# Modulation sums moved ahead of the mixers, and x normalised a tile every seven units

## The chip, the cores and the metric

The kernel runs on one core of one Trainium2 chip. The metric is device time in microseconds (us) of one execution; lower is better. The engines are named as the profile names them: PE (TensorE matmuls) with its weight loads PEld, DVE (VectorE), ACT (ScalarE), POOL (GpSimd), SP (SyncE, which issues DMAs).

## The reference

A decoder trunk of two layers on 256 positions of width 1024, all in float32. Each layer has three sub-layers: a SwiGLU feed-forward, a mixer (even layer: pooling beside differential attention; odd layer: a chunkwise mLSTM), and a second SwiGLU. Each sub-layer has an RMS norm whose shift and scale, and a residual gate, come from a conditioning vector c:

```python
def modnorm(x, g, shift, scale):
    return rmsnorm(x, g) * (1 + scale[:, None, :]) + shift[:, None, :]
...
for l in range(DEPTH):
    mod = (c_act @ w_mod[l] + b_mod[l]).reshape(B, N_SUB, 3, D_MODEL)
    shift, scale, gate = mod[:, :, 0], mod[:, :, 1], mod[:, :, 2]
    h = modnorm(x, norm_g[l, 0], shift[:, 0], scale[:, 0])
    x = x + 0.5 * gate[:, 0, None, :] * swiglu(h, w_ffn_gate[l, 0], w_ffn_up[l, 0], w_ffn_down[l, 0])
    h = modnorm(x, norm_g[l, 1], shift[:, 1], scale[:, 1])
    ...                                       # y = even_mixer(h, ...) or odd_mixer(h, ...)
    x = x + gate[:, 1, None, :] * y
    h = modnorm(x, norm_g[l, 2], shift[:, 2], scale[:, 2])
    x = x + 0.5 * gate[:, 2, None, :] * swiglu(h, w_ffn_gate[l, 1], w_ffn_up[l, 1], w_ffn_down[l, 1])
return rmsnorm(x, final_g)
```

So beside the layers' own matrices there is a modulation: 2 x 9 x 1024 dot products of length 1024 with silu(c).

## The kernel before

x lies transposed: eight tiles of 128 channels by 256 positions. All weights are cut into blocks of 128 by 128 and stand in memory in the order of use. One block is a **unit**; 16 units are a **chunk** of 1 MB, 8 units a **half**. A unit is three matmuls (mm3, lines 341 to 343): the weight's high part by x's high part, low by high, high by low, because both are split into a rounded high part and a remainder to keep float32 accuracy. The 160 chunks run in this order: feed-forward 1 (chunks 0 to 32, of which 0 to 21 are gate and up, 22 to 32 down), even mixer (33 to 40 input blocks, 41 to 44 output), feed-forward 2 (45 to 77, down from 67), feed-forward 3 (78 to 110, down from 100), odd mixer (111 to 122, 123 to 126), feed-forward 4 (127 to 159). In the profiled execution they begin at 17.7, 212.5, 301.7, 491.1, 679.3 and 795.3 us.

`split_to` (line 286) is called from each unit and stays two halves ahead (`look`): it asks SP for the next chunk (line 294), has ACT round a half into wh (line 299) and DVE subtract it into wl (line 300). wh and wl have four buffers each, the raw chunks five.

The **modulation** is summed on DVE: `mod_chunk` (line 242) loads two rows of w_mod blocks (1 MB, tile rawm, line 249) into the same five raw buffers, and `mod_sums` (line 260) makes two sums of 128 x 1024 products (line 267), always directly behind the second half of the chunk in front of which the load was asked for. How many of the 72 loads have been asked for by which chunk is told by the table `MOD_POINTS`, between whose points `mod_schedule` draws straight lines; 8 are made by hand at the start. So chunks 22 to 32, for instance, come with 8 loads.

A new stage begins before x's statistics are known. The last residual of the old stage (`residual`, line 460) at once writes xh and xl, x times the scale column, and the first blocks (`early`: 2 x `NEARLY` of them, so 10) are multiplied by these raw tiles. Two extra columns carry the shift, so their matmuls are 258 columns wide, and the result must be multiplied by the positions' factor `rext` when it leaves PSUM: DVE does so (tile t, line 512, in a feed-forward; tile ti, line 618, in a mixer). `stats_lane` (line 421) runs beside the units: 15 units into the stage the sum of squares is turned into the factor, 7 units later it is spread over the partitions, and from then on a tile of x is normalised every 4 units (`norm_x`, line 442: a product on DVE into xn, a rounding on ACT and a remainder on DVE into xs). Blocks that are not early read xs and are 256 columns wide. The blocks are swept with the last tile of x late for the first two (`sweep`, line 62): these two go over seven tiles each before they need the eighth.

Within a stage small generators (heads, gates, pooling) are stepped at given unit counts. In the odd mixer lf, col and dg are small columns of the gates' chain, each made on DVE (lines 798, 804, 822) and read by PE (lines 801, 808, 827); `head_qk` (line 853) multiplies a head's scores by their decay on DVE (line 866) before PE goes on in the same bank (line 868).

## Time and profile before

| | us |
|---|---|
| three runs | 993.95, 998.08, 998.33 |
| their median | 998.08 |
| the profiled execution | 998.09 |
| its span in the profile | 996.4 |

In a window's row each engine has its busy time and the number of instructions. Matmuls are pipelined, so that of PE not the busy time but the number of matmuls in a window tells the pace. A row of the waits tells which engine's instruction was late for which other one, summed over a window. Of one instruction the profile gives a duration; where instructions follow each other closely, the next one may start a little before the end of the one before, so start to start is the better measure of a queue.

### The profile page before, as it was taken

The page shows a single profiled execution, that of the slowest core. Times are in us where ns is not written, and L with a number is a line of the kernel's source. Part 1 is how long each engine was busy: PE and PEld are TensorE (multiplying, and loading weights), DVE is VectorE, ACT ScalarE, POOL GpSimd, SP SyncE. Part 2 cuts the span into 40 slices and gives each one's busy share as a digit, 9 for nine tenths or more (in the row PEclk, how much of TensorE's full clock was granted, in tenths as well). Part 3 has the DMA queues.
Part 4 walks back from the last instruction along what each step waited for, and adds up shares of the span by engine and source line. Part 5 has one row for each costly group of instructions (what it writes and reads, how often), then busy time and mean ns, then how long its engine had stood idle before and what let it go on. Part 6 is the DMA issues. An engine that isn't in the chain of part 4 may idle for free.

```text
span 996.4 us, 19641 instructions
## 1 busy us (share of the span) xinstructions
PE 973.5 (98%) x8032; PEld 958.8 (96%) x8032; DVE 758.1 (76%) x1201; ACT 528.0 (53%) x872; POOL 217.9 (22%) x223
## 2 busy tenths in 40 slices
PE   7999999999999999999999999999999999999996
PEld 6899999999999999999999999999899999999996
DVE  5979998989879876777798676788867988555452
ACT  3475544448766544444465444445767655444441
POOL 4953220110112322211122222001010113222011
PEclk9999999999999999999999999999999999999998
DMA  9978888875846766766758766676565746565521
GB/s 341 317 295 318 328 329 319 341 284 206 298 155 246 271 245 254 277 252 235 290 182 291 288 245 248 269 293 258 200 223 185 280 171 244 205 229 175 187 105 43
DMA packets 36093, 247.18 MB, mean 248 GB/s; under 512 B 4001, under 2 KB 4385, under 8 KB 7458
## 3 DMA queue, kind: packets, MB, share of 16 engines
q1 hardware_dynamic: 35856, 245.81, 66.7%
q8 instruction: 63, 1.03, 0.4%
q14 instruction: 28, 0.23, 0.1%
q10 hardware_dynamic: 146, 0.11, 0.0%
HBM read 244.86 MB, written 1.05 MB: 247 GB/s over the span
## 4 chain that ended last, share of the span: by engine, by line
PE 82%; DVE 9%; ACT 3%; issue 3%; POOL 1%; DVEq 0%; ACTq 0%; POOLq 0%
PE one L343 26%; PE one L341 26%; PE one L342 26%; DVE wl L300 3%; DVE rawm L267 3%; ACT wh L299 1%; DVE xs L447 1%; POOL hr L401 1%; DVE xn L445 1%; PE one L418 0%; DVE xl L587 0%; DVE t L512 0%; DVE h L490 0%; ACT L488 0%; PE one L842 0%
## 5 line engine op out<-in xcount | busy, mean ns | idle before, releaser
L300 DVE TENSOR_TENSOR wl<-raww,wh 128x1024 fp32r<-128x1024 f32 x320 | 395.5, 1239 | 162.4 <-ACT wh L299 161.1
L299 ACT ACTIVATE wh<-raww 128x1024 fp32r<-128x1024 f32 x320 | 337.2, 1056 | 226.7 <-PE one L343 197.3
L341 PE MATMUL one<-xs,wh 128*128 128x256 f32 x976 | 275.3, 282 | 0.0
L342 PE MATMUL one<-xs,wl 128*128 128x256 f32 x976 | 272.9, 280 | 1.0 <-DVE wl L300 1.0
L343 PE MATMUL one<-xs,wh 128*128 128x256 f32 x976 | 273.1, 280 | 0.0
L341 PE MATMUL one<-hid,wh 128*128 128x256 f32 x832 | 233.7, 281 | 0.2 <-ACT hid L601 0.2
L343 PE MATMUL one<-hid,wh 128*128 128x256 f32 x832 | 233.7, 281 | 0.0
L342 PE MATMUL one<-hid,wl 128*128 128x256 f32 x832 | 233.3, 280 | 0.0
L342 PE MATMUL one<-xh,wl 128*128 128x258 f32 (+1 forms) x752 | 207.5, 285 | 3.2 <-DVE wl L300 2.9
L341 PE MATMUL one<-xh,wh 128*128 128x258 f32 (+1 forms) x752 | 208.1, 287 | 1.8 <-ACT xh L585 1.8
L343 PE MATMUL one<-xl,wh 128*128 128x258 f32 (+1 forms) x752 | 204.6, 283 | 0.0
L493 POOL TENSOR_TENSOR hid<-h,hid 128x256 fp32r<-128x256 f32 x88 | 123.3, 1402 | 340.1 <-ACT hid L492 340.1
L342 PEld LDWEIGHTS one<-xs,wl 128*128 128x128 f32 x976 | 183.6, 188 | 1.4 <-DVE wl L300 1.2
L341 PEld LDWEIGHTS one<-xs,wh 128*128 128x128 f32 x976 | 183.0, 187 | 1.2 <-issue 1.0
L343 PEld LDWEIGHTS one<-xs,wh 128*128 128x128 f32 x976 | 183.1, 188 | 0.0
L341 PEld LDWEIGHTS one<-hid,wh 128*128 128x128 f32 x832 | 156.8, 188 | 0.4 <-ACT hid L601 0.4
L343 PEld LDWEIGHTS one<-hid,wh 128*128 128x128 f32 x832 | 156.6, 188 | 0.2 <-DVE hid L602 0.2
L342 PEld LDWEIGHTS one<-hid,wl 128*128 128x128 f32 x832 | 156.7, 188 | 0.0
L267 DVE CUSTOM_DVE_ANT_0 rawm<-rawm,cact,pk 128x1024 f32<-128x1024 f32 x112 | 150.5, 1371 | 0.0
L342 PEld LDWEIGHTS one<-xh,wl 128*128 128x128 f32 x752 | 140.6, 191 | 5.4 <-DVE wl L300 5.2
L341 PEld LDWEIGHTS one<-xh,wh 128*128 128x128 f32 x752 | 140.3, 191 | 4.1 <-ACT xh L585 2.3
L343 PEld LDWEIGHTS one<-xl,wh 128*128 128x128 f32 x752 | 138.8, 189 | 0.2 <-DVE xl L587 0.2
(222 smaller groups left out, 727.0 us busy)
## 6 DMA issues: line engine op xcount, KB each, us to landing
raww<-wst SPq DMA_DIRECT2D x152, 1024.0 KB, 4.8
rawm<-mst SPq DMA_DIRECT2D x71, 1024.0 KB, 4.9
raww<-wst SPq DMA_DIRECT2D x16, 512.0 KB, 6.4
xa<-xT SPq DMA_DIRECT2D x2, 512.0 KB, 4.7
rawm<-mst SPq DMA_DIRECT2D x2, 512.0 KB, 7.4
outT<-fin SPq DMA_DIRECT2D x3, 256.0 KB, 2.8
pk<-pack SPq DMA_DIRECT2D x1, 416.0 KB, 6.9
outT<-fin SPq DMA_DIRECT2D x2, 128.0 KB, 2.3
```

The source lines that it names most:

```text
L267: nc.vector.tensor_tensor_reduce(out=ri, in0=ri, in1=cact, scale=factor, scalar=first, op0=ALU.mult, op1=ALU.add, accum_out=modc[n // KT][ ...
L299: nc.scalar.activation(whs[i], src, AF.Copy)
L300: ins = nc.vector.tensor_tensor(out=wls[i], in0=src, in1=whs[i].bitcast(F32), op=ALU.subtract)
L341: nc.tensor.matmul(out, lhsT=wh, rhs=rh, start=start, stop=False, skip_group_check=skip)
L342: nc.tensor.matmul(out, lhsT=wl, rhs=rh, start=False, stop=False, skip_group_check=skip)
L343: nc.tensor.matmul(out, lhsT=wh, rhs=rl, start=False, stop=stop, skip_group_check=skip)
L401: nc.gpsimd.tensor_tensor(out=r, in0=v, in1=mhalf[:, 0:width], op=ALU.pow)
L445: nc.vector.scalar_tensor_tensor(out=xn, in0=x[k], scalar=a, in1=r, op0=ALU.mult, op1=ALU.mult)
L447: nc.vector.scalar_tensor_tensor(out=to[1], in0=xn, scalar=b, in1=to[0].bitcast(F32), op0=ALU.add, op1=ALU.subtract)
L493: nc.gpsimd.tensor_tensor(out=hl[:, 0:T], in0=h, in1=hh[:, 0:T].bitcast(F32), op=ALU.subtract)
```

## The change

Three constants change:

```diff
-NEARLY = 5
+NEARLY = 6
...
-MOD_POINTS = ((8, 8), (41, 32), (72, 44), (104, 56), (124, 68), (145, 72))
+MOD_POINTS = ((8, 8), (20, 18), (33, 31), (45, 32), (78, 47), (111, 68), (145, 72))
...
         for k in range(KT):
-            yield 4
+            yield 7
             norm_x(k, rext[:, 0:T], A_cols[key][:, k:k + 1], shift[:, k:k + 1], xs[k])
```

By the tables, the loads that are asked for in front of the chunks of each stage are:

| chunks | stage | before | now |
|---|---|---|---|
| 0 to 7 | feed-forward 1, start | 8 | 8 |
| 8 to 21 | feed-forward 1, gate and up | 9 | 11 |
| 22 to 32 | feed-forward 1, down | 8 | 11 |
| 33 to 44 | even mixer | 8 | 1 |
| 45 to 66 | feed-forward 2, gate and up | 8 | 10 |
| 67 to 77 | feed-forward 2, down | 4 | 5 |
| 78 to 99 | feed-forward 3, gate and up | 9 | 14 |
| 100 to 110 | feed-forward 3, down | 5 | 7 |
| 111 to 126 | odd mixer | 9 | 2 |
| 127 to 148 | feed-forward 4, gate and up | 4 | 3 |

Twelve blocks of a stage instead of ten are multiplied raw, and the eight tiles of x are normalised over 56 units instead of 32.

Three places show what moves. In the fences, wl is the low part of a half chunk, rawm<-...cact the two sums of a load (the row `mod_... 128x1` behind each only stores it), xa the residual sum into x.

The first is DVE's queue in the first down part. Before, from the first half of chunk 27 to the second of chunk 28:

```order
L300 TENSOR_TENSOR wl_2160<-raww_2157,wh_2159 128x1024
L461 SCALAR_TENSOR_TENSOR xa<-one_2082,mod_122,xa 128x256
L300 TENSOR_TENSOR wl_2198<-raww_2157,wh_2197 128x1024
L392 SCALAR_TENSOR_TENSOR xl_93<-xa,acol_2062,xh_85 128x256
L395 TENSOR_TENSOR xl_98<-mod_123,xh_90 128x2
L300 TENSOR_TENSOR wl_2230<-raww_2227,wh_2229 128x1024
L300 TENSOR_TENSOR wl_2268<-raww_2227,wh_2267 128x1024
L267 ISA rawm_2225,mod_125<-rawm_2225,cact,pk 128x1024
L267 ISA mod_125 128x1
```

Now, from the first half of chunk 27 to the first of chunk 28:

```order
L300 TENSOR_TENSOR wl_2174<-raww_2171,wh_2173 128x1024
L300 TENSOR_TENSOR wl_2212<-raww_2171,wh_2211 128x1024
L267 ISA rawm_2169,mod_126<-rawm_2169,cact,pk 128x1024
L267 ISA mod_126 128x1
L267 ISA rawm_2169,mod_127<-rawm_2169,cact,pk 128x1024
L267 ISA mod_127 128x1
L461 SCALAR_TENSOR_TENSOR xa<-one_2192,mod_122,xa 128x256
L368 SCALAR_TENSOR_TENSOR acol_3631<-mod_127,pk 128x1
L300 TENSOR_TENSOR wl_2246<-raww_2243,wh_2245 128x1024
```

Chunk 27 had no load in front of it, and the splits of chunks 27 and 28 followed each other with only a residual and its remainders between; now a load's two sums stand behind each chunk's splits, as for all chunks from 16 to 33.

The second is DVE's queue at the start of feed-forward 2, ahead of the split for the first half of chunk 50 (the last row in both; t is a raw block's evacuation, xs and xn are halves of a tile's normalisation). Before:

```order
L300 TENSOR_TENSOR wl_4156<-raww_4116,wh_4155 128x1024
L447 SCALAR_TENSOR_TENSOR xs_112<-xn_4128,mod_126,xs_111 128x256
L447 SCALAR_TENSOR_TENSOR xs_114<-xn_4144,mod_126,xs_113 128x256
L267 ISA rawm_4114,mod_128<-rawm_4114,cact,ghalf 128x1024
L267 ISA mod_128 128x1
L267 ISA rawm_4114,mod_128<-rawm_4114,cact,ghalf 128x1024
L267 ISA mod_128 128x1
L512 TENSOR_TENSOR t_4185<-one_4113,rext 128x258
L512 TENSOR_TENSOR t_4185<-one_4154,rext 128x258
L300 TENSOR_TENSOR wl_4200<-raww_4197,wh_4199 128x1024
```

Now:

```order
L490 SCALAR_TENSOR_TENSOR h_4095<-t_4090,sg_4093 128x256
L447 SCALAR_TENSOR_TENSOR xs_106<-xn_4114,mod_126,xs_105 128x256
L300 TENSOR_TENSOR wl_4138<-raww_4102,wh_4137 128x1024
L445 SCALAR_TENSOR_TENSOR xn_4144<-xa,acol_3631,rext 128x256
L512 TENSOR_TENSOR t_4169<-one_4101,rext 128x258
L300 TENSOR_TENSOR wl_4186<-raww_4183,wh_4185 128x1024
```

The two sums and the two remainders that stood between the second half of chunk 49 and that split now come behind it; a product and one evacuation are left.

The third is DVE's queue in the odd mixer, around the scores of head 3 (line 866). Before:

```order
L300 TENSOR_TENSOR wl_9368<-raww_9365,wh_9367 128x1024
L399 TENSOR_SCALAR hv_9319<-dss_9310 128x2
L908 TENSOR_TENSOR hr_9321<-hr_9321,dr_9309 128x2
L300 TENSOR_TENSOR wl_9433<-raww_9365,wh_9432 128x1024
L866 SCALAR_TENSOR_TENSOR hid_9410<-one_9407,hid_9082 128x256
L871 TENSOR_TENSOR hid_9414<-hid_9250,hid_9083 128x128
```

Now:

```order
L399 TENSOR_SCALAR hv_9347<-dss_9338 128x2
L908 TENSOR_TENSOR hr_9349<-hr_9349,dr_9337 128x2
L300 TENSOR_TENSOR wl_9461<-raww_9393,wh_9460 128x1024
L267 ISA rawm_9391,mod_137<-rawm_9391,cact,ghalf 128x1024
L267 ISA mod_137 128x1
L866 SCALAR_TENSOR_TENSOR hid_9438<-one_9435,hid_9114 128x256
L267 ISA rawm_9391,mod_137<-rawm_9391,cact,ghalf 128x1024
L267 ISA mod_137 128x1
L871 TENSOR_TENSOR hid_9442<-hid_9280,hid_9115 128x128
```

The scores' product stood directly behind a split; now one of a load's two sums stands between them.

## Rows read from the trace of the kernel before

**Rows 1.** The profile's page: busy time of two engines (us, share of the span, instructions), and the chain that ended last by engine, as shares of the span.

```profile
PE 973.5 (98%) x8032; PEld 958.8 (96%) x8032; DVE 758.1 (76%) x1201; ACT 528.0 (53%) x872; POOL 217.9 (22%) x223
...
PE 82%; DVE 9%; ACT 3%; issue 3%; POOL 1%; DVEq 0%; ACTq 0%; POOLq 0%
```

**Rows 2.** Busy time of the engines in windows of the span (from:to in us, length, then busy us and instructions of PE, PE's weight loads, DVE, ACT and POOL, the granted clock, the DMA engines' share, GB/s). They are, in this order, feed-forward 1's gate and up blocks from chunk 8 on; its down part; the even mixer's input blocks; feed-forward 2's gate and up; its down part; feed-forward 3's gate and up; the odd mixer's input blocks.

```profile
74.00:150.34 76.34, 76.34 (x647) 76.34 (x646) 70.77 (x98) 39.91 (x60) 22.13 (x18) 1.00 0.85 324
150.34:212.54 62.20, 62.20 (x531) 62.20 (x529) 54.63 (x82) 29.22 (x38) 6.17 (x7) 1.00 0.84 320
212.54:273.63 61.09, 60.52 (x487) 57.06 (x485) 55.33 (x119) 44.63 (x114) 6.48 (x5) 1.00 0.71 257
...
301.73:428.80 127.07, 126.07 (x1066) 125.86 (x1065) 100.16 (x147) 67.03 (x101) 33.37 (x24) 1.00 0.69 254
428.80:491.14 62.34, 62.34 (x531) 62.34 (x529) 45.45 (x63) 28.80 (x37) 6.61 (x7) 1.00 0.67 254
491.14:616.96 125.82, 125.82 (x1066) 125.82 (x1065) 97.70 (x146) 65.33 (x98) 31.90 (x23) 1.00 0.71 259
...
679.31:772.57 93.26, 90.63 (x715) 85.93 (x714) 70.37 (x165) 63.11 (x137) 5.44 (x6) 1.00 0.59 214
```

**Rows 3.** Waits of PE (engine and line, who ended the wait: us in total, times, longest us) in four windows, in this order: 212.54 to 301.73 us (even mixer), 300 to 335 (start of feed-forward 2), 679 to 773 (odd mixer), 795 to 825 (start of feed-forward 4).

```profile
PE one L710 <- ACT hid L705: 0.6, 1, 0.6
PE one L341 <- ACT hid L601: 0.2, 1, 0.2
...
PE one L342 <- DVE wl L300: 1.0, 1, 1.0
...
PE one L868 <- DVE hid L866: 1.7, 1, 1.7
PE one L827 <- DVE dg L822: 0.4, 1, 0.4
PE one L808 <- DVE col L804: 0.3, 1, 0.3
PE one L801 <- DVE lf L798: 0.2, 1, 0.2
...
PE one L342 <- DVE wl L300: 1.3, 1, 1.3
```

**Rows 4.** DVE in order of time, 327 to 333 us, around the wait at the start of feed-forward 2 (start us, duration us, engine, line, operation, out<-in, how many).

```profile
327.08 1.36 DVE L447 SCALAR_TENSOR_TENSOR xs<-xn,mod,xs 128x256 fp32r<-128x256 f32 x2
328.36 1.27 DVE L267 CUSTOM_DVE_ANT_0 rawm<-rawm,cact,ghalf 128x1024 f32<-128x1024 f32 x1
...
329.57 1.27 DVE L267 CUSTOM_DVE_ANT_0 rawm<-rawm,cact,ghalf 128x1024 f32<-128x1024 f32 x1
...
330.78 0.74 DVE L512 TENSOR_TENSOR t<-one,rext 128x258 f32<-128x258 f32 x2
331.45 1.21 DVE L300 TENSOR_TENSOR wl<-raww,wh 128x1024 fp32r<-128x1024 f32 x1
332.58 0.47 DVE L490 SCALAR_TENSOR_TENSOR h<-t,sg 128x256 f32<-128x256 f32 x1
```

**Rows 5.** Groups of equal instructions over the whole span (line, engine, operation, tiles and shapes, count | busy us, mean ns of one | idle time ahead of them and what ended it).

```profile
L299 ACT ACTIVATE wh<-raww 128x1024 fp32r<-128x1024 f32 x320 | 337.2, 1056 | 226.7 <-PE one L343 197.3 <-issue 17.3 <-DMA raww<-wst 6.5
...
L392 DVE SCALAR_TENSOR_TENSOR xl<-xa,acol,xh 128x256 fp32r<-128x256 f32 x40 | 31.6, 796 | 3.1 <-ACT xh L391 2.9
...
L445 DVE SCALAR_TENSOR_TENSOR xn<-xa,acol,rext 128x256 f32<-128x256 f32 x40 | 17.9, 478 | 0.0
...
L512 DVE TENSOR_TENSOR t<-one,rext 128x258 f32<-128x258 f32 x30 | 11.7, 416 | 0.7 <-ACT rext L429 0.7
```

**Rows 6.** DVE in order of time in the odd mixer, at two places: 701 to 703 us and 747 to 749 us (in brackets the idle time ahead of the instruction and what ended it).

```profile
701.19 1.28 DVE L267 CUSTOM_DVE_ANT_0 rawm<-rawm,cact,pk 128x1024 f32<-128x1024 f32 x1
...
702.87 0.16 DVE L798 SCALAR_TENSOR_TENSOR lf<-gt,ln 128x8 f32<-128x8 f32 x1
...
747.82 1.23 DVE L300 TENSOR_TENSOR wl<-raww,wh 128x1024 fp32r<-128x1024 f32 x1 [1.91 <-ACT wh L299]
748.97 0.42 DVE L866 SCALAR_TENSOR_TENSOR hid<-one,hid 128x256 f32<-128x256 f32 x1
```

**Rows 7.** Two windows of three chunks each in the gate and up part of feed-forward 3: its third to fifth chunk, read raw and 258 columns wide, and three later chunks of 256 columns (columns as in rows 2).

```profile
503.64:520.89 17.25, 17.25 (x147) 17.25 (x146) 17.25 (x32) 12.24 (x21) 5.18 (x4) 1.00 0.54 196
526.54:543.49 16.95, 16.95 (x147) 16.95 (x146) 13.51 (x19) 8.32 (x12) 5.20 (x4) 1.00 0.86 309
```

**Rows 8.** The DMA queue: the queue's own waits for the sums over the whole span (us in total, times, longest us); from issue to landing of the weight chunks that line 294 asks for between 140 and 215 us; and GB/s in 40 equal slices of the first down part (150.34 to 212.54 us, so 1.55 us a slice).

```profile
SPq L294 <- DVE mod L267: 100.2, 41, 4.4
...
DMA to landing us min/median/max: 4.7/5.1/6.4
...
GB/s 395 316 369 379 253 21 248 432 411 332 353 395 421 126 221 421 416 406 416 126 63 385 348 427 232 432 400 411 306 390 285 427 432 200 0 227 437 427 300 211
```

**Rows 9.** DVE in order of time: the residual of the first down part's last tile, whose last matmul ends at 212.54 us (columns as in rows 4).

```profile
213.33 0.47 DVE L461 SCALAR_TENSOR_TENSOR xa<-one,mod,xa 128x256 f32<-128x256 f32 x1
```

**Rows 10.** The sums of line 267 in two windows, 74 to 150.34 us (gate and up of feed-forward 1) and 679.31 to 772.57 us (odd mixer): count, then ns of one as least/median/most, first and last start, shape.

```profile
L267 DVE CUSTOM_DVE_ANT_0 rawm<-rawm,cact,pk x12: 1274/1516/1768, 107.7 to 149.2; 128x1024 f32<-128x1024 f32 x12
...
L267 DVE CUSTOM_DVE_ANT_0 rawm<-rawm,cact,pk x14: 1276/1278/1284, 688.0 to 771.5; 128x1024 f32<-128x1024 f32 x14
```

## The prediction

> **What bounds the kernel now.** The page first: TensorE (PE) is busy for 98% of the span, and the chain of waits that ended last goes through PE for 82% and through VectorE (DVE) for 9% [rows 1]. PE's busy share alone proves little, since matmuls overlap, so the second view is the stages: in the down projections (150 to 213 us and 429 to 491 us, 11 weight chunks each) PE issues 531 matmuls in 62.2 to 62.3 us, which is 5.65 us a chunk whatever DVE does beside it, and the granted clock is 1.00 throughout [rows 2]. The kernel is therefore an even stream of 160 chunks that only loses time where PE waits for another engine. The third view lists those waits [rows 3]. At the start of feed-forward 2 (300 to 335) PE waits 1.0 us for the low half of a weight split, at the start of feed-forward 4 (795 to 825) 1.3 us, in the odd mixer 1.7 + 0.4 + 0.3 + 0.2 = 2.6 us, in the even mixer 0.6 + 0.2 = 0.8 us. Together that is **5.7 us**, and it is all that an edit to DVE's order can win after the start-up, which the change leaves alone (both tables begin with 8 loads by chunk 8).
>
> DVE is the engine that can lose time. It holds its busy share at 70.8 of 76.3 us (93%) in the gate and up part of feed-forward 1 and at 54.6 of 62.2 us (88%) in its down part; in the odd mixer it is at 70.4 of 93.3 us [rows 2]. The change moves work from the latter to the former.
>
> **The price of a modulation load.** One load is 1 MB on the DMA queue and two sums on DVE. A sum takes 1.27 us by its row, but the next instruction starts 1.21 us after it (328.36, 329.57, 330.78) [rows 4], so I use 2.4 us for the pair. A split costs 1.13 us from start to start (331.45 to 332.58) [rows 4], one product or addition of normalising a tile of x 0.48 us by its row [rows 5], about 0.40 us back to back.
>
> **Part 1, fewer sums in the mixers.** By the tables the mixers' 28 chunks carry 3 loads in place of 17. In the odd mixer 14 sums become 4, so DVE loses 10 x 1.21 = 12.1 us of its 70.4. The wait of 0.2 us for lf goes with that, since a sum of 1.2 us stands directly ahead of the end of its chain (701.19) [rows 6]. The waits for col and dg (0.3 and 0.4 us) stay: what stands ahead of them are splits and normalised tiles, and the slower pace puts more of these beside that chain. The longest, 1.7 us for the scores of head 3 (L866), stays too: DVE idles 1.91 us for the high half of a weight split, takes the low half in 1.23 us (747.82) and only then turns to L866 [rows 6], and no sum is in that queue. In the changed order one sum stands between them. I price that at +0.3 us, bounds 0 and the whole sum of 1.2 us. In the even mixer 14 of 16 sums leave (8 loads become 1); what waits there is a power on POOL and a scaling on ScalarE behind DVE's statistics, of which I take half: 0.4 us. Gain of this part: 0.2 + 0.4 - 0.3 = 0.3 us.
>
> **Part 2, x normalised every 7 units.** Around 330 us a pair of sums, the last normalised tiles and two evacuations stand directly ahead of the split that PE waits for [rows 4]. In the changed order only one product and one evacuation are between that split and the one before, and the two sums of the next load come after it. That is 2.4 us of DVE less ahead of a wait of 1.0 us, so the wait goes. In feed-forward 4 the load falls ahead of the stage's own rush, and its 1.3 us go as well. Gain 2.3 us; bounds 0 (the delayed work makes the next split late in its place) and 2.3. The last tile of x is due at 15 + 7 + 8 x 7 = 78 units and is first read at unit 96 (before: 54 and 80), so PE has 18 units of 0.353 us, 6.4 us, of cover: no wait.
>
> **Part 3, twelve raw blocks instead of ten.** A raw block's matmuls are 258 columns wide. Three chunks of them take 17.25 us, three chunks of 256 columns 16.95 us, with 147 matmul records in both windows [rows 7]: 0.1 us a chunk. Two more blocks are one more chunk in each of five stages: **+0.5 us on PE**, bare. DVE gets ten more evacuations of 0.42 us by their rows [rows 5], hidden by its idle time (27 of 127 us in feed-forward 2's gate and up part, [rows 2]); without cover 4.2 us.
>
> **Part 4, more sums in the stages in front.** Chunks 8 to 21 get 11 loads instead of 9: DVE 70.8 + 2 x 2.4 = 75.6 of 76.3 us. Chunks 22 to 32 get 11 instead of 8: 54.6 + 7.2 = 61.8 of 62.2 us. DVE is full, not over. Chunks 78 to 99 get 14 instead of 9: 97.7 + 12.0 = 109.7 of 125.8; covered by the same slices' idle time, price 0, bounds 0 and 1.0 (the wait at 330 us, [rows 3]).
> What no row shows is one load for every chunk, 18 times running (chunks 16 to 33). Five buffers of 1 MB hold both kinds, so weight chunk c can only be asked for when the sums of the load two chunks earlier are done. The queue's own waits show this already: 100.2 us for sums, 41 times [rows 8]. Then it must land, 4.7, 5.1 or 6.4 us (least, median, most) in this stretch [rows 8], and be rounded by ScalarE in 1.06 us [rows 5]. So from one pair of sums to the split two chunks on: 0.1 + 5.1 + 1.06 = 6.3 us. From there DVE needs two splits, a pair of sums and one product, 5.1 us, in chunks 16 to 21, and 5.65 with the residuals in 22 to 33 (the 61.8 us above). Two chunks per 11.4 and 11.95 us are 5.70 and 5.98 us a chunk, 0.05 and 0.33 over PE's pace: 6 x 0.05 + 12 x 0.33 = 4.3 us behind at the end. Cover: a high half may start when PE leaves the half four earlier, 3 x 2.83 = 8.5 us before it is due, less 1.06 + 1.13, so 6.3 us. At the median PE does not starve. But the residual of the last tile comes late by the same amount: before, it ran 0.8 us after the stage's end (213.33 against 212.54) [rows 9]; PE reads that tile 14 units or 4.9 us into the mixer, and the residual (0.4 us), its rounding (some 0.5, as a product) and the remainder (0.8) [rows 5] with their hand-overs need about 2 us, so 2.9 us are free. 4.3 less the 1 us by which DVE was ahead is 3.3, a stall of 0.4 us. With every landing at 4.7 us the loop costs 12 x 0.13 = 1.6 us, no stall. At 6.4 us it costs 6 x 0.7 + 12 x 0.97 = 15.8 us, so 9.5 us of starving and 3.4 us at the mixer's start: 12.9. I take **+1.0 us** (the median's 0.4 and 0.6 for the busier queue), bounds 0 and 12.9.
>
> Sums are dearer where they go to. In the gate and up part of feed-forward 1, beside POOL's 22.1 us of work, a sum takes 1.27 to 1.77 us with a median of 1.52; in the odd mixer, with 5.4 us of POOL in 93.3, all 14 take 1.28 [rows 2, 10]. Four sums at 1.70 from start to start are 6.8 us in place of 4.8, and DVE would be at 77.6 of 76.3 us in chunks 8 to 21. The Trainium skill's page SBUF — State Buffer (Who interferes with whom) has a rule for it that speaks against the change: a VectorE instruction with two SBUF inputs and a GpSimd instruction that reads SBUF share one interface, and the later one waits for the whole of the other. The rows agree as far as they go. At the price of the quiet stretches, which I take since half of the sums here pay no more, the sum stays as it is; at the full price it is rival (c).
>
> **The sum.** It is made against the profiled execution, 998.09 us, which is at the median of the three runs (998.08; the lowest 993.95). 998.1 - 2.3 - 0.6 (gains of parts 2 and 1) + 0.3 + 0.5 + 1.0 = **997.0 us**. A difference of under 0.5%, some 5 us, is about what a measurement of this kernel cannot tell from no change.
>
> **The rivals.** (a) All waits go, nothing new comes: 998.1 - 5.7 + 0.5 = 992.9. For it: every one of them ends at DVE or just behind it, and DVE is lighter in all four places. Against: the largest, 1.7 us, has no sum in its queue. Chance 0.20.
> (b) Slower: the buffer loop of chunks 16 to 33. If landings grow with the load on the queue, from 320 to 371 GB/s (2 x 1.049 MB in 5.65 us), towards the 6.4 us that the trace has as the longest, the price is 12.9 us: 998.1 - 2.9 + 0.3 + 0.5 + 12.9 = 1008.9. It decides from a mean landing of 5.33 us, where 6 x ((5.33 + 1.2 + 5.1) / 2 - 5.65) + 12 x ((5.33 + 1.2 + 5.65) / 2 - 5.65) reaches the cover of 6.3 us. Against: single slices of 1.55 us in this stretch moved 432 to 437 GB/s [rows 8], and PE does not wait in it now. Chance 0.13.
> (c) Every moved sum pays for POOL: DVE enters chunk 22 later by 77.6 - 76.3 = 1.3 us, is 4.3 + 1.3 = 5.6 us behind at the end, under the cover of 6.3, and the mixer's start loses 5.6 - 1 - 2.9 = 1.7 us: 997.0 - 1.0 + 0.6 (the same small allowance) + 1.7 = 998.3. (It is what the page's rule would do.) For it: the longest sums, 1.77 us, lie in all gate and up parts. Chance 0.07.
> (d) The change does not do what it says: the waits at the feed-forward starts reappear one split later, with the late tiles and the next load's sums in the queue: 997.0 + 2.3 = 999.3. Chance 0.05.
> My forecast of 997.0 has 0.55.
>
> **How the numbers follow.** Forecast, (c) and (d) are within 0.5% (993.1 to 1003.1): 0.55 + 0.07 + 0.05 = 0.67 same. (a) is just over the bound: 0.20 faster. (b): 0.13 slower. The range runs from 992, which takes in (a), to 1003, which leaves out most of (b) and the lower edge of what the runs themselves scatter.
>
> **What would show it.** Right: 5.65 us a chunk in the first down part; no wait of L342 for a low half at the starts of the third and the last feed-forward; raw chunks up by one in five stages; the wait for L866 still there. Wrong: landings over 5.33 us between 130 and 212 us with PE waiting for a low half there or at the even mixer's first blocks (b); L866 gone (a); a wait one or two splits after unit 80 of a stage (d). The forecast fails as a whole if PE's 5.65 us a chunk itself moves, which no row gives a reason for.

## The result and the profile after

The changed kernel takes 1007.04 us (median of 4 runs, 1005.45 to 1007.32) against 998.13 us (4 runs, 993.95 to 998.33): 1.0096 times as long, 95% interval 1.0068 to 1.0125. That is slower, and outside the range of 992 to 1003. The profiled execution took 1006.77 us with a span of 1005.1 us; before it was 998.09 and 996.4 us. On record, runs of the kernel before lie near 994 or near 998 us (6 of 15 near 994 beside e1 to e4, at most 1 of 13 beside the later runs); what parts the two isn't known.

First the page after: busy time of two engines, and the chain that ended last by engine, which answers to [rows 1].

```profile
PE 978.9 (97%) x8032; PEld 962.2 (96%) x8032; DVE 767.2 (76%) x1211; ACT 527.0 (52%) x872; POOL 209.5 (21%) x223
...
PE 70%; DVE 19%; ACT 5%; issue 5%; POOL 1%; DVEq 0%; ACTq 0%; POOLq 0%
```

PE is busy for 5.4 us and DVE for 9.1 us more than before, about 1% each, but DVE's share of the chain went from 9% to 19%. So it is hardly more work; PE waits for DVE more often. Windows by stage, in the columns of [rows 2], say where. They are the gate and up part of feed-forward 1 from chunk 8 on, its down part, the even mixer's input, the gate and up parts of feed-forward 2 and 3, the odd mixer's input and the gate and up part of feed-forward 4:

```profile
74.69:151.13 76.44, 75.97 (x641) 75.75 (x640) 68.76 (x107) 36.94 (x57) 18.82 (x17) 1.00 0.89 332
151.13:218.49 67.36, 63.87 (x530) 62.73 (x529) 63.20 (x92) 29.45 (x40) 8.30 (x7) 1.00 0.89 341
218.49:281.40 62.91, 62.72 (x487) 58.17 (x485) 48.23 (x111) 45.01 (x115) 4.43 (x5) 1.00 0.49 185
309.49:436.37 126.88, 126.17 (x1066) 125.96 (x1065) 105.40 (x158) 66.60 (x100) 31.45 (x24) 1.00 0.72 265
498.71:625.75 127.04, 126.18 (x1067) 125.97 (x1065) 113.83 (x178) 65.95 (x98) 29.35 (x23) 1.00 0.81 299
688.10:783.24 95.14, 91.68 (x714) 87.22 (x713) 60.76 (x147) 63.82 (x138) 4.53 (x6) 0.98 0.43 153
805.97:931.86 125.89, 125.89 (x1067) 125.89 (x1066) 84.73 (x110) 65.96 (x99) 30.84 (x24) 1.00 0.56 204
```

The lengths (the first number behind the window) against [rows 2]: the first down part **+5.2 us** (62.2 to 67.4), the even mixer's input +1.8 (61.1 to 62.9), feed-forward 2 -0.2, feed-forward 3 +1.2, the odd mixer's input +1.9 (93.3 to 95.1). Chunks 0 to 21 add 0.8 and feed-forward 4 gives back 2.0 (1.5 of them in its gate and up part, which took 127.36 us before). Together 8.7 us, the difference of the spans. The down part is the one to explain first.

PE's waits over the whole span (us in total, times, longest); the last of these rows is read further below:

```profile
PE one L342 <- DVE wl L300: 7.2, 14, 0.9
...
PE one L868 <- DVE hid L866: 2.2, 1, 2.2
...
PE one L808 <- DVE col L804: 1.0, 1, 1.0
```

The wait for the low half of a split is now the largest, 14 short ones; five of them, 3.5 us, lie in the first down part, where there were none. (Such a wait is counted from the end of the matmul ahead. From start to start of the matmuls the places of these waits, and one at chunk 26, cost 5.0 us, which is nearly all of the 5.2.) The wait for L866 grew from 1.7 to 2.2 us [rows 3].

What happens in that part is seen in DVE's queue in order of time, first of the kernel before, then after, around the first two residuals of line 461:

```profile
162.96 1.23 DVE L300 TENSOR_TENSOR wl<-raww,wh 128x1024 fp32r<-128x1024 f32 x1 [0.49 <-ACT wh L299]
164.10 1.28 DVE L267 CUSTOM_DVE_ANT_0 rawm<-rawm,cact,pk 128x1024 f32<-128x1024 f32 x1
...
165.30 1.28 DVE L267 CUSTOM_DVE_ANT_0 rawm<-rawm,cact,pk 128x1024 f32<-128x1024 f32 x1
...
166.51 0.88 DVE L461 SCALAR_TENSOR_TENSOR xa<-one,mod,xa 128x256 f32<-128x256 f32 x2
167.30 1.22 DVE L300 TENSOR_TENSOR wl<-raww,wh 128x1024 fp32r<-128x1024 f32 x1
```

```profile
161.37 2.34 DVE L300 TENSOR_TENSOR wl<-raww,wh 128x1024 fp32r<-128x1024 f32 x2
163.64 1.27 DVE L267 CUSTOM_DVE_ANT_0 rawm<-rawm,cact,pk 128x1024 f32<-128x1024 f32 x1
...
164.85 1.27 DVE L267 CUSTOM_DVE_ANT_0 rawm<-rawm,cact,pk 128x1024 f32<-128x1024 f32 x1
...
167.59 0.88 DVE L461 SCALAR_TENSOR_TENSOR xa<-one,mod,xa 128x256 f32<-128x256 f32 x2 [1.47 <-PE one L343]
168.38 2.35 DVE L300 TENSOR_TENSOR wl<-raww,wh 128x1024 fp32r<-128x1024 f32 x2
170.65 1.77 DVE L267 CUSTOM_DVE_ANT_0 rawm<-rawm,cact,pk 128x1024 f32<-128x1024 f32 x1
```

The rows look alike, but they are one chunk apart. Counting the splits, the last one ahead of the residuals is that of chunk 25's second half before (162.96) and that of chunk 24's second half after (the second in the row at 161.37). After the change DVE waits 1.47 us for the end of PE's block while the split of chunk 25, which PE needs next, stands behind that wait; PE then waits 0.3 us for it. This order is fixed when the kernel is built. How far DVE is ahead of PE at a split (its end, against PE's first matmul on that low half; both starts and ends are in the trace) shows how it came to that:

```
split of   before: end, PE's start, lead    after: end, PE's start, lead (us)
c16.8      113.43, 119.22, 5.79             115.91, 120.02, 4.11
c19.8      130.68, 136.27, 5.59             134.13, 137.06, 2.93
c22.8      147.55, 153.28, 5.73             153.13, 155.01, 1.88
c25.0      162.12, 167.46, 5.34             169.60, 169.66, 0.06
```

(c16.8 is the second half of chunk 16.) Before, the lead at second halves stays near 5.7 us, where the four buffers of the halves hold DVE back. After, it melts by about 0.4 us a chunk from chunk 16 on, and from chunk 25 to 32 it is 0.25 us or less at the first half of every chunk. Both kernels come out of the start-up with a lead of 0.06 us (chunk 8) and are alike up to chunk 11; then the loads of chunks 10 to 14, five running (chunk 12 had none before), take it back to 0.06 us at the first half of chunk 14 (4.64 before), where PE waits 0.5 us. Chunk 15, the only one from 10 to 33 without a load, gives back 2.1 us. DVE's waits in the gate and up part (74 to 150 us before, 74.69 to 151.13 after) and ScalarE's in the same windows, before and after in turn:

```profile
DVE wl L300 <- ACT wh L299: 2.6, 5, 1.0
...
DVE wl L300 <- ACT wh L299: 7.2, 9, 1.4
...
ACT hid L492 <- DVE h L490: 6.2, 10, 1.6
...
ACT hid L492 <- DVE h L490: 22.4, 13, 3.3
```

One such chain after the change (DVE's and ScalarE's rows together in order of time) ends in the split of chunk 22, for which PE then waits 0.6 us, the first wait of the down part and ahead of any residual:

```profile
147.71 1.28 DVE L267 CUSTOM_DVE_ANT_0 rawm<-rawm,cact,pk 128x1024 f32<-128x1024 f32 x1
...
148.92 0.41 DVE L490 SCALAR_TENSOR_TENSOR h<-one,sg 128x256 f32<-128x256 f32 x1
...
149.36 0.42 ACT L492 ACTIVATE hid<-h 128x256 fp32r<-128x256 f32 x1 [3.26 <-DVE h L490]
149.69 1.99 ACT L299 ACTIVATE wh<-raww 128x1024 fp32r<-128x1024 f32 x2
...
150.77 2.36 DVE L300 TENSOR_TENSOR wl<-raww,wh 128x1024 fp32r<-128x1024 f32 x2 [1.10 <-ACT wh L299]
```

Sums delay DVE's product h; ScalarE waits for h (22.4 us in place of 6.2) with the rounding of the next half behind it; DVE then waits for that rounding (7.2 in place of 2.6). A DVE at 90% of its time is late here although it is not full, since part of its idle time lies behind its own work.

### The profile page after: what moved, and what is told of

Same layout as the page of the kernel before. It is cut to its first block, busy times and chain, and to the rows that moved or that the text cites. A ratio compares the mean times of both kernels' runs of the same rounds, so it can differ in the third digit from the quotient of the medians.

```text
span 1005.1 us, 19676 instructions
## 1 busy us (share of the span) xinstructions
PE 978.9 (97%) x8032; PEld 962.2 (96%) x8032; DVE 767.2 (76%) x1211; ACT 527.0 (52%) x872; POOL 209.5 (21%) x223
## 4 chain that ended last, share of the span: by engine, by line
PE 70%; DVE 19%; ACT 5%; issue 5%; POOL 1%; DVEq 0%; ACTq 0%; POOLq 0%
PE one L342 22%; PE one L341 22%; PE one L343 22%; DVE wl L300 7%; DVE rawm L267 7%; ACT wh L299 3%; DVE h L490 1%; DVE xs L447 1%; DVE xn L445 1%; DVE t L512 1%; PE one L418 0%; POOL hid L493 0%; DVE xl L587 0%; ACT hid L492 0%; PE one L664 0%
## 5 line engine op out<-in xcount | busy, mean ns | idle before, releaser
L341 PE MATMUL one<-xs,wh 128*128 128x256 f32 x896 | 253.1, 282 | 0.0
L342 PE MATMUL one<-xs,wl 128*128 128x256 f32 x896 | 251.3, 280 | 1.6 <-DVE wl L300 1.6
L343 PE MATMUL one<-xs,wh 128*128 128x256 f32 x896 | 250.9, 280 | 0.0
L342 PE MATMUL one<-xh,wl 128*128 128x258 f32 (+1 forms) x832 | 230.2, 285 | 2.5 <-DVE wl L300 2.2
L341 PE MATMUL one<-xh,wh 128*128 128x258 f32 (+1 forms) x832 | 231.2, 287 | 1.4 <-ACT xh L585 1.4
L343 PE MATMUL one<-xl,wh 128*128 128x258 f32 (+1 forms) x832 | 227.1, 283 | 0.0
L342 PEld LDWEIGHTS one<-xs,wl 128*128 128x128 f32 x896 | 168.9, 189 | 2.1 <-DVE wl L300 2.0
L341 PEld LDWEIGHTS one<-xs,wh 128*128 128x128 f32 x896 | 168.8, 188 | 0.5 <-issue 0.3
L343 PEld LDWEIGHTS one<-xs,wh 128*128 128x128 f32 x896 | 168.5, 188 | 0.0
L342 PEld LDWEIGHTS one<-xh,wl 128*128 128x128 f32 x832 | 156.1, 191 | 4.7 <-DVE wl L300 4.5
L341 PEld LDWEIGHTS one<-xh,wh 128*128 128x128 f32 x832 | 155.6, 191 | 4.2 <-issue 2.3
L343 PEld LDWEIGHTS one<-xl,wh 128*128 128x128 f32 x832 | 154.0, 189 | 0.2 <-DVE xl L587 0.2
```

The source lines that it names most:

```text
L341: nc.tensor.matmul(out, lhsT=wh, rhs=rh, start=start, stop=False, skip_group_check=skip)
L342: nc.tensor.matmul(out, lhsT=wl, rhs=rh, start=False, stop=False, skip_group_check=skip)
L343: nc.tensor.matmul(out, lhsT=wh, rhs=rl, start=False, stop=stop, skip_group_check=skip)
```

## The experiments

Each ratio is against runs of the kernel before on the same chip. The two stretches at issue, and the whole time, stand side by side behind the first nine; the table of loads is called the table. In the cuts of code, ... stands for lines left out.

**Which edit.** The table alone, taken out of the change (e1, whose edit is shown) and put alone into the kernel before (e2, the reverse edit):

```
-MOD_POINTS = ((8, 8), (20, 18), (33, 31), (45, 32), (78, 47), (111, 68), (145, 72))
+MOD_POINTS = ((8, 8), (41, 32), (72, 44), (104, 56), (124, 68), (145, 72))
```

> The changed kernel with the old table of loads alone (12 raw blocks and a tile of x every 7 units stay). If the table does the harm (theory T, the loop of five buffers in chunks 16 to 33), the first down part goes back from 67.4 to 62.2 us (within 0.5) with no wait for a low half in it, and the whole time is 997 to 1000 us: 1007 less 5.2 for the down part, less 1 to 3 us for the odd mixer and feed-forward 3, where the table moved loads too. If the twelve blocks or the slower tiles do it (rival), the time stays above 1004 us.

995.56 us, ratio 0.9989 (0.9976 to 1.0002), 1.4 us under the range expected; down part 62.2 us. The two other edits alone are harmless: feed-forward 2's and 4's gate and up parts fall from 127.1 and 127.4 to 125.9 us each.

> The kernel before with the new table alone (10 raw blocks, a tile of x every 4 units). Theory T: the first down part takes 66 to 68 us in place of 62.2, and the whole time is 1003 to 1008 us. Rival (the other two edits do it): 996 to 1000 us, down part under 63 us.

1005.19 us, ratio 1.0082 (1.0056 to 1.0108); down part 67.4 us. The whole loss is the table's.

**Buffers, bytes or DVE.**

```
-    raw_pool = ctx.enter_context(tc.tile_pool(name="raw", bufs=5))
+    raw_pool = ctx.enter_context(tc.tile_pool(name="raw", bufs=6))
...
```

> The changed kernel with six buffers of 1 MB in place of five; the room comes from single buffers for the attention's scores and the square sums, one buffer less for its transposes and 44 in place of 46 hidden tiles, so only the first feed-forward (to chunk 32) is read, and the mixers may lose. Loop of buffers (theory T): a weight chunk can be asked for one more chunk ahead, the first down part falls from 67.4 to under 63.5 us and PE's waits for a low half in it go. DVE simply full (rival F: 61.8 of 62.2 us of work, dearer sums): the extra buffer gives DVE no time, the down part stays at 66.5 us or more. Landings themselves too slow for the bytes (rival B, 371 GB/s wanted): stays at 66.5 or more, with landings longer than the 6.0 us median.

1006.13 us, ratio 1.0104 (1.0076 to 1.0132). The down part, and PE's wait in it:

```profile
151.19:218.55 67.36, 63.81 (x530) 62.67 (x529) 63.23 (x92) 29.01 (x40) 8.32 (x7) 1.00 0.88 341
...
PE one L342 <- DVE wl L300: 3.5, 5, 0.9
```

The median landing of the weight chunks from 140 to 220 us fell from 6.0 to 4.9 us and ScalarE's waits for them from 12.1 to 1.8 us, and PE's five waits did not move. The loop of buffers, which the prediction had as its slow rival, is not the cause. It was real, but hidden.

> The changed kernel with loads of half the bytes: one column of each pair is loaded and both sums read it, so half of the modulation is left out and the output is another; DVE's work stays the same. Theory T and rival B: fewer bytes land sooner (median raw landing from 6.0 to under 4.8 us), so the first down part falls to 62.2 to 63.5 us. Rival F (DVE full): the sums are as many and as long, so it stays at 66.5 us or more.

```
-        w = 2048 // parts
+        w = D // parts
...
-                ri = r[:, i * D:(i + 1) * D]
+                ri = r[:, 0:D]
...
-                    out=ri, in0=ri, in1=cact, scale=factor, scalar=first,
+                    out=r[:, (1 - i) * D:(2 - i) * D], in0=ri, in1=cact, scale=factor, scalar=first,
```

1005.43 us, ratio 1.0097 (1.0067 to 1.0128). The down part came to 62.2 us, as expected for bytes; but the even mixer's first two chunks took 20.4 us in place of 15.5 after and 14.9 before, part of it at a lower granted clock (0.83 over the two). In this kernel's order on DVE the residuals stand one chunk later again, so PE gets its splits and the residuals are late. Its chunks 0 to 7 also take 3.1 us longer, and DVE comes to the first half of chunk 22 with a lead of 3.0 us in place of 0.05. The loss changed its place, and the run does not tell bytes from DVE.

> The changed kernel with sums over 512 of the 1024 columns (half of each sum is left out, so the modulation is another); loads, table, blocks and tiles stay. Theory F (DVE full in the first down part: 63.2 us of work in 11 chunks of 5.65): 22 sums of some 0.68 us in place of 1.30 take 13.6 us from DVE, so the first down part takes 62.2 us (within 0.3), the wait for L866 behind a sum shrinks from 2.2 to 1.6 to 1.8 us without the low clock after it, the wait at the start of feed-forward 3 goes, and the time is 994 to 999 us. Rival B (bytes): the queue carries as much as before, so the down part stays over 65 us.

```
-                    out=ri, in0=ri, in1=cact, scale=factor, scalar=first,
+                    out=ri[:, 0:512], in0=ri[:, 0:512], in1=cact[:, 0:512], scale=factor, scalar=first,
```

1006.15 us, ratio 1.0081 (1.0066 to 1.0096), missed: the start-up takes 5.3 us longer (chunks 7 and 8, PE waits 3.8 us for roundings), and the down part falls only to 65.0 us, with DVE busy for 48.2 of them. Theory F alone does not hold. The lead melts here too, from 6.1 us at the first half of chunk 16 to 1.9 at that of chunk 22, although ScalarE hardly waits for h there (1.2 us from 118 to 155 us, against 9.1 after the change): the length of the sums is not all that melts it. The wait at the start of feed-forward 3 went as expected. The wait for L866 stayed at 2.2 us: in this kernel PE has less to do ahead of it (two units of work between lines 864 and 868 in place of three).

> The changed kernel with both reliefs: six buffers of 1 MB (room as in the run with six buffers) and sums over 512 of the 1024 columns (half of each sum is left out). Six buffers alone left the first down part at 67.4 us, half sums alone brought it to 65.0. If DVE's work is the first limit and the loop of buffers the second (theory FT), both together give 62.2 to 63.0 us. If the bytes of 11 loads and 11 chunks in that time are the second limit (371 GB/s wanted, 343 measured with half sums), it stays at 64 us or more.

1004.31 us (2 runs), ratio 1.0064 (1.0045 to 1.0082); 64.95 us in the down part. By its expectation this speaks for the bytes, which e14 below rules out. Neither buffers nor DVE's work is what is left. DVE waited 10.9 us there for ends of PE's blocks, five times, each with splits behind it: the order.

> The changed kernel with the splits asked for three halves ahead of PE in place of two (the four buffers of high and low halves allow it), all else as it is. In the first down part DVE is busy for 63.2 of 67.4 us and idle for 5.2 us with the stretch's ends, 2.0 of it at residuals that wait for PE's block. Theory G (DVE's queue order: a residual that waits for PE holds back the splits that PE needs next): with splits a half, 2.8 us, earlier the down part falls to 62.2 to 65 us. Theory F in its bare form (63.2 us of work is the limit): it falls to 63.5 to 64.5 us at best, since DVE can save idle time only. If it stays at 67 us, neither the place of the splits nor their lead counts. Time 1001 to 1006 us by G and F.

```
-        look[0] = 2
+        look[0] = 3
```

1006.75 us, ratio 1.0086 (1.0072 to 1.0100); down part 67.4 us. Asking earlier changed nothing, since the first residuals kept their place, behind the split of chunk 24's second half: theory G was not put to the test. What counts is the order that the build settles on, not the one the code asks in.

> The changed kernel with one constraint: every residual stands on DVE behind the last split asked for ahead of it, which puts the first two behind the split of chunk 25's second half, as before the change, in place of chunk 24's. Table, sums, loads and buffers as in the changed kernel. Theory Q (the queue's order alone): the first down part falls to 62.2 to 63 us and the even mixer's input part stays at 62.9, time 1001 to 1003 us. Theory F (DVE's work alone: it is a few us behind whatever stands first): PE gets its splits in time and the residuals are late instead, so the down part falls to 62.2 to 63.5 and the even mixer's first two chunks take 3 to 5 us more than 15.5 us, as with loads of half the bytes; time 1004 to 1007 us.

```
+            last_split[0] = ins
...
-        nc.vector.scalar_tensor_tensor(out=x[n], in0=ps, scalar=modc[(l * NSUB + s) * 3 + 2][:, n:n + 1], in1=x[n],
-                                       op0=ALU.mult, op1=ALU.add)
+        with tc.issue_after(last_split[0].ins):
+            nc.vector.scalar_tensor_tensor(out=x[n], in0=ps, scalar=modc[(l * NSUB + s) * 3 + 2][:, n:n + 1],
+                                           in1=x[n], op0=ALU.mult, op1=ALU.add)
```

1005.58 us, ratio 1.0078 (1.0061 to 1.0095). The time is in theory F's range, but the down part is in neither's:

```profile
151.36:216.11 64.75, 63.36 (x530) 62.57 (x529) 60.83 (x91) 27.67 (x39) 5.98 (x7) 1.00 0.94 356
216.11:280.12 64.01, 62.87 (x486) 58.28 (x485) 49.32 (x111) 46.47 (x116) 4.42 (x5) 1.00 0.50 181
```

The rows are the down part and the even mixer's input. 2.6 us come back in the down part, and 1.1 of them are lost again in the mixer: the constraint is worth 1.5 us. It is not the wait for PE alone that it takes away: of DVE's instructions in the down part that are longer beside POOL (rival (c) below) there are four in place of seven, some 1.4 us less of DVE's time. This pair of runs doesn't part the two. DVE is still idle for 3.9 us, nearly all behind ScalarE.

> The same constraint with sums over 512 of the 1024 columns (half of each sum is left out). With half sums alone the down part was 65.0 us. If order and work are the two causes and nothing else is (Q and F together), the down part takes 62.2 to 62.5 us and the even mixer's input part 62.2 us, as with half sums. If the bytes of a load for every chunk are a third limit, the down part stays over 63.5 us or the mixer's first chunks grow.

1001.93 us, ratio 1.0045 (1.0030 to 1.0060), with the longer start-up of the half sums in it:

```profile
154.60:216.89 62.29, 62.29 (x530) 62.29 (x529) 49.30 (x91) 29.13 (x39) 5.17 (x7) 1.00 0.97 371
216.89:279.12 62.23, 62.23 (x486) 58.05 (x485) 45.92 (x109) 44.92 (x114) 4.44 (x5) 1.00 0.48 178
```

The two stretches together are within 0.8 us of the kernel with the old table, at 371 GB/s and with five buffers. So order and work of DVE are the two causes in this part, and bytes are no third one. For the order the pair e5 and e14 is the clean one: 2.7 us (127.3 to 124.5), with DVE's 8.9 us of waits for ends of PE's blocks gone and its time lost beside POOL nearly the same (1.6 and 1.4 us). In the work there is one thing not parted: with half sums the longer start-up gives DVE a larger lead (1.9 us at the first half of chunk 22 in place of 0.05), and how much of the relief comes from that is not shown. Chunks 22 to 40 side by side:

```
kernel                           down part + mixer input (us)   whole time
before                           62.2 + 61.1 = 123.3             998.1
changed                          67.4 + 62.9 = 130.3            1007.0
old table (e1)                   62.2 + 61.5 = 123.7             995.6
new table alone (e2)             67.4 + 61.5 = 128.9            1005.2
six buffers (e3)                 67.4 + 62.9 = 130.3            1006.1
half the bytes (e4)              62.2 + 67.7 = 129.9            1005.4
half sums (e5)                   65.0 + 62.2 = 127.3            1006.2
both reliefs (e9)                65.0 + 62.3 = 127.2            1004.3
splits asked for earlier (e10)   67.4 + 63.7 = 131.0            1006.8
residuals behind (e13)           64.8 + 64.0 = 128.8            1005.6
residuals behind, half sums (e14) 62.3 + 62.2 = 124.5           1001.9
```

**The even mixer.** Its 1.8 us come with hardly any wait (0.4 us). The first two chunks take 0.6 us more, with the residuals late, and chunk 38 0.8 less, without the wait of L710. The rest, 2.0 us, is two of the four heads: they have their ten score matmuls (six calls in the code; each 64-row call is two records) in another order on PE. PE in order of time at the second head, before and then after:

```profile
233.45 0.52 PE L660 MATMUL one<-masks,identr 128*128 128x384 f32 x2
233.90 0.50 PE L662 MATMUL one<-hid,hid 64*128 64x128 f32 x4
234.22 0.61 PE L664 MATMUL one<-hid,hid 64*128 64x256 f32 x4
234.76 0.39 PE L341 MATMUL one<-xh,wh 128*128 128x258 f32 x1
```

```profile
240.04 0.34 PE L660 MATMUL one<-masks,identr 128*128 128x384 f32 x1
240.31 0.49 PE L662 MATMUL one<-hid,hid 64*128 64x128 f32 x2
240.63 0.59 PE L664 MATMUL one<-hid,hid 64*128 64x256 f32 x2
241.16 0.44 PE L660 MATMUL one<-masks,identr 128*128 128x384 f32 x1
241.53 0.48 PE L662 MATMUL one<-hid,hid 64*128 64x128 f32 x2
241.85 0.59 PE L664 MATMUL one<-hid,hid 64*128 64x256 f32 x2
242.37 0.39 PE L341 MATMUL one<-xh,wh 128*128 128x258 f32 x1
```

Four 64-row matmuls take the time of two where both halves of the rows follow each other: 1.31 us a head against 2.33. Before, one head had the one order whole, one had it with the masks apart, and two had the other; after the change all four have the other.

> The changed kernel with the ten score matmuls of a head issued with the two row halves in turn (mask, mask, then the 64-row matmuls of half 0 and half 1 next to each other). Theory O (the order in which they stand sets their cost): every head takes 1.31 us from the first of them to the next unit as in chunk 35 before, in place of 2.29 us, so the even mixer's input part falls from 62.9 us by 3 to 4 us and the time to 1002.5 to 1004 us. Rival: the difference between the two orders is an effect of when DVE delivers the heads; then less than 1 us is won.

```
+            rows = [slice(64 * c, 64 * c + 64) for c in range(2)]
+            for c in range(2):
+                nc.tensor.matmul(pp[c][:, 0:3 * P], lhsT=identr, rhs=masks3, start=True, stop=False,
+                                 skip_group_check=True)
+            for c in range(2):
+                nc.tensor.matmul(pp[c][:, 0:P], lhsT=q[rows[c], 0:P], rhs=kk[rows[c], 0:P], start=False, stop=True,
+                                 skip_group_check=True)
+            for c in range(2):
+                nc.tensor.matmul(pp[c][:, P:3 * P], lhsT=q[rows[c], P:T], rhs=kk[rows[c], 0:T], start=False,
+                                 stop=True, skip_group_check=True)
```

1003.01 us, ratio 1.0048 (1.0033 to 1.0063) to the kernel before: the mixer's input falls from 62.9 to 58.8 us, about 1 us for each of the four heads. Theory O holds.

**Only the first part undone, and a better table.**

> The changed kernel with the old table up to chunk 41 and the new one from 45 on: only the loads moved into the first feed-forward are undone. Theory F: the first down part goes back to 62.2 us and the part before it to 132.7, which is 6.0 us of the 8.7 lost; the waits in feed-forward 3 (1.1 us) and at L866 (2.2 us and the low clock) stay. Time 999.5 to 1001.5 us. If it comes to 997 or less, the odd mixer's loss hangs on the first part too; if it stays over 1004, the first part is not the cause.

999.45 us, ratio 1.0010 (0.9997 to 1.0022): 62.2 us in the down part. The wait for L866 stayed at 2.2 us, and feed-forward 2 and 3 still lost 1 us each at their starts. The low clock behind L866 did not come in the profiled execution (below).

> Twelve raw blocks, a tile of x every 7 units, score matmuls in turn as in the run with the heads, and another table: the old one up to chunk 78, then 49 loads by chunk 85 and 68 by chunk 111, none in the odd mixer. Theory F with O: first down part 62.2 us; no new wait at the start of feed-forward 3, since the steep part begins after the rush of x; the wait for L866 stays 1.7 us (no sum in its queue) and the clock stays at 1.00 behind it; the even mixer's input part 58.5 us. Time 990 to 993 us. If moved sums cost wherever they go (rival), feed-forward 3 grows by over 2 us and the time is 995 us or more.

993.95 us, ratio 0.9961 (0.9946 to 0.9975). Every stage as expected but for 0.6 us at chunk 84 and 0.4 us at the mixer's end, and so the time is 1 us over its range.

> As the run with the late table (score matmuls in turn, 12 blocks, 7 units), with two points moved: 28 loads in place of 26 by chunk 33, four in place of six in the even mixer, and the steep part of feed-forward 3 from chunk 87 on. Theory F: the down part of feed-forward 1 carries 9 loads and stays at 62.2 us (54.6 + 2.4 = 57 of 62.2 us of DVE); the wait of 0.6 us at chunk 84 goes, and the even mixer's last wait of 0.4 us as well. 991.5 to 993.5 us against 993.95 for the late table.

993.47 us, ratio 0.9947 (0.9934 to 0.9961). Both waits went, and one came at chunk 51 that cost 1.0 us. Nine loads in the first down part cost nothing; eleven cost 5 us. In this table a load stands in front of four chunks of five, and at each fifth the lead comes back: at second halves from 3.3 us (chunk 19) to 5.9 (chunk 20), from 4.0 (chunk 29) to 5.5 (chunk 30).

> As the run before it, with one more edit: the scores of head h in the odd mixer are asked for 2h in place of 4h units after the gates are ready, which puts the scores' product of head 3 on DVE ahead of the split that it stood behind. Theory W (the wait of 1.7 us is DVE's order: a split that waits 1.9 to 2.2 us for its high half stands ahead of the product): the wait falls under 0.5 us, the odd mixer's input part from 93.2 to 91.5 to 92.2 us. Rival: PE waits as long for the split that is now behind, and nothing is won.

```
-            yield 4 * h
+            yield 2 * h
```

992.93 us, ratio 0.9951 (0.9938 to 0.9963). The odd mixer's input fell only from 93.3 to 92.9 us, and the wait is 1.4 us: the rival had most of it.

> As the run with the scores earlier, with the table's 32 loads due at chunk 41 in place of 45, as in the first late table, where feed-forward 2 had no wait at its start (126.9 us with it, 125.9 without). Its even mixer had a wait of 0.4 us at the end for it, with six loads in it; four should leave none. 991.5 to 992.5 us if both hold, 993 if the waits only change places.

```
-MOD_POINTS = ((8, 8), (20, 18), (33, 31), (45, 32), (78, 47), (111, 68), (145, 72))
+MOD_POINTS = ((8, 8), (33, 28.1), (41, 32), (78, 46), (87, 49), (111, 68), (127, 68), (145, 72))
```

992.02 us (6 runs, 991.63 to 992.44), ratio 0.9945 (0.9934 to 0.9957): the lowest median of all, though by the intervals not clear of e11 and e12. The first down part, the even mixer's input, feed-forward 3's gate and up part and the odd mixer's input:

```profile
150.44:212.63 62.19, 62.19 (x530) 62.19 (x529) 56.38 (x83) 29.68 (x39) 5.18 (x7) 1.00 0.88 338
212.63:270.90 58.27, 58.27 (x487) 55.93 (x485) 53.22 (x127) 44.85 (x114) 5.57 (x5) 1.00 0.64 239
487.23:613.14 125.91, 125.91 (x1066) 125.91 (x1065) 111.91 (x174) 65.86 (x98) 30.90 (x23) 1.00 0.79 293
675.50:768.19 92.69, 90.06 (x715) 85.84 (x713) 58.92 (x145) 63.87 (x138) 4.37 (x6) 1.00 0.41 148
```

## Why the prediction was wrong

**Part 4 failed**, at "DVE is full, not over". It priced the down part's 61.8 us of DVE work against 62.2 us and found room. The busy time came to 63.2 us, 1.0 us over what PE needs there. The larger term that the sum left out is time in which DVE can't work: it waits for ScalarE's roundings and for PE's block ends (4.2 us idle there, by 67.4 less 63.2, and 7.2 us behind ScalarE in the part before, where DVE was busy for 68.8 us, not the 75.6 that were priced, and fell behind all the same). The cover of 6.3 us was counted as whole at chunk 16; the loads of chunks 10 to 14 had used it up before, and the lead was 4.1 us there. The melting was priced at 0.05 us a chunk in chunks 16 to 21 and was about 0.4 (from a lead of 4.1 to 1.9 us between the second halves of chunks 16 and 22). The second miss of this part is the order: the residuals' new place in DVE's queue could be read ahead of the run, and was not looked at around chunk 25. +1.0 us was forecast for feed-forward 1 and +6.0 came. In feed-forward 3 the five loads more were priced at 0, at most 1.0, and cost 1.1 us at chunk 84.

**Rival (b)** gave 1008.9 us and named this part, but its mechanism fell: a sixth buffer takes the landings away and leaves the wait (e3). The landings did pass its 5.33 us, at 6.0 us in the median, and did not decide. With the order mended and the sums halved, PE is fed at 371 GB/s (e14). A time near the measured one had the wrong reason.

**Part 1** was forecast as 0.3 us of gain. The even mixer's wait of L710 went as said, but two of its four heads lost their order on PE (1 us each), which no part considered; e6 shows that it is the order. In the odd mixer the wait for lf went, that for dg too (it was to stay), and the sum ahead of L866 cost 0.5 us, within its bounds of 0 and 1.2. The wait for col grew from 0.3 to 1.0 us in place of staying. Another 1.6 us is the clock behind L866: its chunk takes 12.4 us, against 10.8 in e8 with the same wait at full clock.

**Part 2** was right in its mechanism: with the old table both waits go (e1). In the changed kernel the one in feed-forward 4 went, and the one in feed-forward 2 came back at the next chunk, which is rival (d); e11 and e15 differ there by the table's phase alone (126.9 and 125.9 us).

**Part 3** was right: the one chunk more takes 5.75 in place of 5.65 us in feed-forward 2, 3 and 4; in the mixers' uneven chunks it can't be read.

**Rival (c)** had the mechanism half right. In the down part no split was longer than 1.23 us before; after the change five took 1.64 to 1.76 us and one sum 1.77 (one is the last row of the second queue above), and each of them began while an instruction of POOL was still running. That is six times 0.5 us, five of them on splits and not on the moved sums it priced; in chunks 8 to 21, 21 of 22 sums took 1.27 to 1.28 us. Nor is it all new: before, five of the seven remainders of line 392 in the down part took 0.95 to 0.97 us in place of 0.48, after the change one. So the change costs DVE some 1.0 us here, 3.4 us in place of 2.4. The Trainium skill's page SBUF — State Buffer (Who interferes with whom) has this: a VectorE instruction with two SBUF inputs contends with a GpSimd instruction that reads SBUF, and which of them was issued first decides which one waits. The trace agrees by its starts: splits in the same stretch that began ahead of POOL's instruction took 1.21 to 1.23 us, and the six grew by 0.42 to 0.54 us where POOL's had 0.56 to 0.68 us left. What this 1.0 us does to PE by itself is not shown; with the residuals behind later splits (e13) it is gone, together with their wait for PE.

**Rival (a)** fell.

What stays open: why the clock fell behind L866 in some executions only, how much of the loss in the down part is the wait for PE and how much the work where sums are whole, and how much of DVE's idle time behind ScalarE an order of ScalarE's queue could take back.

## What to carry to other kernels

Price work moved to a busy engine against the time that it can use, not against the span: count its waits for engines that wait for itself, and follow its lead over the consumer from chunk to chunk. A chunk without the added work gives the lead back (e11), so leave some. Where a scheduler settles each engine's order at build time, read that order wherever load changes, the stretches without waits first of all: an instruction that must wait for the consumer, put ahead of what the consumer needs, costs more than its length. And a rival with the right time can have the wrong mechanism, so undo the mechanism (here one buffer more) before believing it.

## What the runs showed of the hardware

- Four 64-row matmuls on the two halves of the rows run in pairs if the halves follow each other (starts 13 ns apart), and one after another if one half's stand together and a 128-row matmul comes between them and the other's: ten matmuls in 1.31 us against 2.33, 4.1 us in the whole mixer (e6).
- After a gap of 2.5 us between two matmul starts in the odd mixer, PE's granted clock was 0.58 on average over 4 us, so mostly at its level of 1.2 GHz, and 1.00 (2.4 GHz) again behind it. Windows ahead of the gap, behind it and after that:

```profile
751.40:756.40 5.00, 5.00 (x45) 5.00 (x45) 1.63 (x4) 3.79 (x10) 0.69 (x1) 1.00 0.00 0
759.40:763.40 4.00, 3.98 (x21) 3.98 (x22) 3.27 (x6) 2.33 (x6) 0.00 (x0) 0.58 0.92 371
763.60:767.40 3.80, 3.80 (x33) 3.75 (x32) 1.44 (x2) 1.99 (x4) 0.00 (x0) 1.00 0.33 136
```

  The same gap in e8 left it at 1.00, with 33 matmuls in 4 us. Of the eleven profiled executions with a gap of 2.4 to 2.6 us there, seven had the lower clock behind it (after, e2, e4, e5, e6, e10, e13) and four not (e3, e8, e9, e14); in those with a gap of 1.6 to 2.0 us (before, e1, e7, e11, e12, e15) it stayed at 1.00.
